# Two late stores of a batched matmul, each issued as three transfers over 112, 12 and 4 or 112, 8 and 8 partitions

## The chip, the core and the metric

The kernel runs on one core of a Trainium2 chip. The metric is the device time of one execution in microseconds, median of several executions. The core has a matrix engine (PE, whose weight loads are listed as PEld), three engines for elementwise work (DVE, ACT, POOL), a synchronising engine (SP), from whose queue all but one of this kernel's transfers are issued, and 16 DMA engines that carry out each transfer together. "DMA engine" below always means one of these 16.

## The reference

```python
def setup_inputs():
    batch, m, k, n = 16, 512, 1024, 768
    # x (16,512,1024), weight (1024,768), bias (768), residual (16,512,768), all float32, standard normal

def reference(x, weight, bias, residual):
    return (np.matmul(x, weight) + bias + residual).astype(np.float32)
```

So 8192 rows of x, each 1024 long, go through one 1024 x 768 weight; a bias row and a residual of the size of the output are added. In and out of the device memory go 33.6 MB of x, 3.1 MB of weight, 25.2 MB of residual and 25.2 MB of output.

## The kernel before

**Tiles.** The 8192 rows are cut into 64 tiles of 128 rows, eight tiles to a group, so there are eight groups g = 0 to 7. In a group each of the 128 partitions holds eight consecutive rows (`group`, "(p j) k -> p j k"): a partition of a group is one contiguous piece of 24,576 bytes in the output and the residual, and of 32,768 bytes in x. A group's store is therefore 128 pieces of 24,576 bytes, eight for each DMA engine.

**Work on one tile.** For tile t: ACT casts x to bf16 (`cast_x`, L121), PE transposes eight 128 x 128 blocks (L136), DVE copies them out of the accumulator memory (L143), PE makes 16 matmuls, eight blocks of the inner dimension times two column chunks of 512 and 256 (L150). DVE adds the residual to the result, in place in the residual's tile (`evacuate`, L167), and POOL adds the bias to it (`add_bias`, L174). The residual's tile then holds the output and is stored from there (`store`, L106). The first tiles are interleaved with the arrival of the weight, and group 0 has a tile of its own for the output; both lie at the other end of the kernel. The last tile is done in two column chunks, each with its own add (L296) and its own store.

**Order.** The order of each engine's instructions is written out by hand. The loop runs over t = 3 to 62; after tile t the dictionary `moves` says which loads and stores SP issues there. SP works its list strictly in order: an issue whose data is not ready holds all issues behind it. The list around the change is: load of residual 7 and store of group 4 (t = 45), store of group 5 (t = 47), store of group 6 (t = 55), and group 7 in five parts: tiles 0 to 3 (t = 59), 4 and 5 (t = 61), 6 (t = 62), then the last tile's 512 and 256 columns. Below they are called store 4, store 5, store 6, and 7a, 7b, 7c, 7d and 7e.

**Memory and waits.** Four places (`HOME`, "ring") hold the residuals in turn. Group 5 has place 2 and group 6 place 0, and no later load goes to either, so no load waits for stores 5 and 6. SP gives its transfers eight completion counters in turn; a transfer may be issued once the transfer eight places before it on SP's list has landed.

Of the kernel before, what the change touches and what calls it, by code (L numbers as in the profile page):

```python
# [10 lines left out]
P = 128  # L11
# [10 lines left out]
def kernel(  # L22
# [8 lines left out]
    nc = tc.nc  # L31
    x2d = x.flatten_outer_dims()
    res2d = residual.flatten_outer_dims()
    out2d = out.flatten_outer_dims()
# [7 lines left out]
    def group(ap, g):  # L42

        return ap[g * G * P:(g + 1) * G * P, :].rearrange("(p j) k -> p j k", p=P)
# [14 lines left out]
    def o(ins):  # L59
        return tc.keep_in_program_order(ins)  # L60
# [26 lines left out]
    x_tiles, r_tiles, o_tiles, w_stage = {}, {}, {}, {}  # L87
# [16 lines left out]
    def store(g, j0=0, j1=G, n0=0, n1=N):  # L104
        src = o_tiles[g] if g == 0 else r_tiles[g]
        o(nc.sync.dma_start(out=group(out2d, g)[:, j0:j1, n0:n1], in_=src[:, j0:j1, n0:n1]))  # L106


    xb_tiles, pt_tiles, xt_tiles, po_tiles = {}, {}, {}, {}
# [114 lines left out]
    for k in range(2, 6):  # L224
# [21 lines left out]
        5: [(load_r, 0), (load_r, 2)],  # L246
        12: [(load_x, 3)],
        15: [(store, 1)],
        17: [(load_r, 3)],
        20: [(load_x, 4)],  # L250
        21: [(load_r, 4), (store, 0)],
        28: [(load_x, 5)],
        29: [(load_r, 5), (store, 2)],
        36: [(load_x, 6)],
        37: [(load_r, 6), (store, 3)],
        44: [(load_x, 7)],
        45: [(load_r, 7), (store, 4)],
        47: [(store, 5)],
        55: [(store, 6)],
        59: [(store, 7, 0, 4)],  # L260
        61: [(store, 7, 4, 6)],
        62: [(store, 7, 6, 7)],
# [63 lines left out]
```

## Time and profile before

| | |
|---|---|
| time, median of 3 executions | 211.54 us (211.37 to 211.62) |
| the profiled execution: its time | 211.21 us |
| the profiled execution: span from the first to the last instruction | 209.4 us |
| granted clock of PE | 1.0 |
| bytes moved, mean rate over the span | 87.28 MB, 417 GB/s |
| store of a whole group: issue to landing, median of six | 23.8 us |
| 7a (1536 KB), 7b (768 KB), 7c (384 KB): issue to landing | 6.5, 5.7, 3.6 us |

A profile describes one execution. Its span is 1.8 us shorter than its time, which also holds what lies before the first and after the last instruction. "Busy" counts the time in which an engine works on an instruction; an engine can be busy all the time and still not be what the end waits for, and the reverse.

The DMA rows count what the 16 DMA engines do together. Behind them stand records of single packets (start, duration, bytes, queue) and, for every transfer, 16 times at which its completion counter rose, one for each DMA engine that has carried its share. Neither names the DMA engine. Since a DMA engine carries one packet after another, the end of one packet and the start of the next can be joined into 16 chains, and so a late DMA engine can be followed from transfer to transfer.

### The profile page before, as it was taken

Reading aid. Unit: us, or ns where it says so; the run is one execution under the profiler, and the core shown is the slowest. Engines: PE = TensorE matmul, PEld = TensorE weight load, DVE = VectorE, ACT = ScalarE, POOL = GpSimd, SP = SyncE. Lnnn points to the kernel's source line nnn. Section 1 sums busy time; section 2 is a strip of 40 time slices with the busy share of each in tenths; the row PEclk is TensorE's granted clock in tenths of the full one; section 3 lists DMA queues with packets and bytes.
Section 4 is the critical chain, followed back from the end, with each engine's and each line's share of the span. In section 5 each row is a group of like instructions: output and inputs, shape, how many; then the busy total and the mean of one; then the engine's idle time right before and its main releaser. Section 6 shows DMA issues by size and latency. Waiting matters only on the chain.

```text
span 209.4 us, 3673 instructions
## 1 busy us (share of the span) xinstructions
PE 199.8 (95%) x1560; PEld 134.1 (64%) x1590; DVE 113.9 (54%) x145; ACT 67.2 (32%) x69; POOL 109.1 (52%) x66
## 2 busy tenths in 40 slices
PE   7797999999999999999999999999999999999992
PEld 7554766666666666666666666666666666666661
DVE  0656555455477745464554454455445545579942
ACT  2633508606331073302632063310743008310000
POOL 2000000275579999966556655655665566554620
PEclk9999999999999999999999999999999999999999
DMA  6999999999999999999999999999999999999895
GB/s 232 402 424 440 448 404 444 419 451 413 418 468 430 410 418 430 443 432 419 427 437 432 426 421 440 444 426 427 413 441 448 426 421 407 437 443 432 355 403 222
DMA packets 5640, 87.28 MB, mean 417 GB/s; under 512 B 628, under 2 KB 756, under 8 KB 2296
## 3 DMA queue, kind: packets, MB, share of 16 engines
q1 hardware_dynamic: 5616, 87.03, 97.8%
q8 instruction: 12, 0.20, 0.4%
q14 instruction: 4, 0.03, 0.0%
q10 hardware_dynamic: 8, 0.01, 0.0%
HBM read 61.88 MB, written 25.17 MB: 416 GB/s over the span
## 4 chain that ended last, share of the span: by engine, by line
PE 88%; DMA 7%; issue 1%; DVE 1%; ACT 0%; SPq 0%; POOL 0%; POOLq 0%
PE po L150 74%; PE pt L136 13%; DMA x_tile<-in_x_dram 5%; DMA bias_rows<-in_bias_dram 3%; PE last_ps L293 1%; DVE xt L143 1%; ACT xb L118 0%; DVE r_tile L296 0%; SPq L97 0%; POOL ident masks.py:197 0%; POOL bias_rows L73 0%; POOLq L310 0%
## 5 line engine op out<-in xcount | busy, mean ns | idle before, releaser
L150 PE MATMUL po<-w_sb,xt 128*128 128x512 bf16 (+1 forms) x978 | 172.2, 324 | 3.2 <-DVE xt L143 1.5
L174 POOL TENSOR_TENSOR r_tile<-r_tile,bias_bc 128x768 f32<-128x768 f32 x53 | 95.7, 1813 | 90.4 <-DVE r_tile L167 90.4
L150 PEld LDWEIGHTS <-xt 128*128 128x128 bf16 x1008 | 95.8, 98 | 59.8 <-DVE xt L143 2.4
L121 ACT CAST xb<-x_tile 128x1024 bf16<-128x1024 f32 x62 | 62.1, 1044 | 109.2 <-DMA x_tile<-in_x_dram 58.2
L167 DVE TENSOR_TENSOR r_tile<-po,r_tile 128x768 f32<-128x768 f32 x55 | 52.6, 956 | 72.5 <-PE po L150 65.0
L143 DVE COPY xt<-pt 128x1024 bf16<-128x1024 bf16 x64 | 43.5, 680 | 3.9 <-PE pt L136 3.8
L136 PEld LDWEIGHTS <-xb 128*128 128x128 bf16 x512 | 35.3, 113 | 9.2 <-ACT xb L118 2.0
L136 PE MATMUL pt<-ident,xb 128*128 128x128 bf16 x512 | 39.0, 219 | 1.4 <-ACT xb L118 1.4
L178 POOL TENSOR_TENSOR o_tile<-o_tile,r_tile 128x768 f32<-128x768 f32 x6 | 12.1, 2056 | 0.0
L164 DVE TENSOR_TENSOR o_tile<-po,bias_bc 128x768 f32<-128x768 f32 x8 | 7.5, 953 | 4.8 <-PE po L150 4.8
L174 DVE TENSOR_TENSOR r_tile<-r_tile,bias_bc 128x768 f32<-128x768 f32 x3 | 6.6, 2189 | 0.0
L202 PE MATMUL warm_ps<-warm_in 128*128 128x128 bf16 x54 | 5.3, 281 | 1.1 <-DVE warm L76 1.1
L202 PEld LDWEIGHTS <-warm_in 128*128 128x128 bf16 x54 | 4.9, 133 | 1.1 <-DVE warm L76 1.1
L119 DVE CAST xb<-x_tile 128x512 bf16<-128x512 f32 x2 | 0.9, 427 | 6.5 <-DMA x_tile<-in_x_dram 6.5
L127 DVE CAST w_sb<-w_stage 128x768 bf16<-128x768 f32 x5 | 2.8, 558 | 2.6 <-DMA w_stage<-in_weight_dram 2.6
L178 DVE TENSOR_TENSOR o_tile<-o_tile,r_tile 128x768 f32<-128x768 f32 x2 | 3.9, 1944 | 0.0
L125 ACT CAST w_sb<-w_stage 128x768 bf16<-128x768 f32 x3 | 2.5, 832 | 4.1 <-DMA w_stage<-in_weight_dram 4.1
L293 PE MATMUL last_ps<-w_sb,xt 128*128 128x512 bf16 (+1 forms) x16 | 2.8, 326 | 0.0
L293 PEld LDWEIGHTS <-xt 128*128 128x128 bf16 x16 | 1.6, 98 | 1.1
L118 ACT CAST xb<-x_tile 128x512 bf16<-128x512 f32 x2 | 1.2, 618 | 3.1 <-DMA x_tile<-in_x_dram 3.1
L77 ACT ACT_TABLE_LOAD x1 | 1.3, 1283 | 2.6 <-POOL ident masks.py:199 2.6
L296 DVE TENSOR_TENSOR r_tile<-last_ps,r_tile 128x512 f32<-128x512 f32 (+1 forms) x2 | 1.1, 558 | 1.0 <-PE last_ps L293 1.0
(12 smaller groups left out, 3.1 us busy)
## 6 DMA issues: line engine op xcount, KB each, us to landing
x_tile<-in_x_dram SPq DMA_DIRECT2D x7, 4096.0 KB, 33.4
r_tile<-in_residual_dram SPq DMA_DIRECT2D x8, 3072.0 KB, 21.3
out_dram<-r_tile SPq DMA_DIRECT2D x6, 3072.0 KB, 23.8
x_tile<-in_x_dram SPq DMA_DIRECT2D x3, 1024.0 KB, 11.8
out_dram<-o_tile SPq DMA_DIRECT2D x1, 3072.0 KB, 31.2
w_stage<-in_weight_dram SPq DMA_DIRECT2D x6, 384.0 KB, 7.2
out_dram<-r_tile SPq DMA_DIRECT2D x1, 1536.0 KB, 6.5
x_tile<-in_x_dram SPq DMA_DIRECT2D x2, 512.0 KB, 8.2
```

The lines of the kernel that those rows point to most:

```text
L121: o(nc.scalar.copy(out=xb_tiles[t], in_=src))
L125: o(nc.scalar.copy(out=w_sb[:, k, :], in_=w_stage[0][:, k, :]))
L127: o(nc.vector.tensor_copy(out=w_sb[:, k, :], in_=w_stage[0][:, k, :]))
L136: o(nc.tensor.transpose(out=pt[:, k, :], in_=xb[:, h, j, :], identity=ident))
L143: o(nc.vector.tensor_copy(out=xt_tiles[t], in_=pt_tiles.pop(t)))
L150: o(nc.tensor.matmul(po_tiles[t][:, n0:n0 + nl], lhsT=xt_tiles[t][:, k, :], rhs=w_sb[:, k, n0:n0 + nl], start=(k == 0), stop=(k == n_k - 1),))
L164: o(nc.vector.tensor_add(out=o_tiles[0][:, j, :], in0=po, in1=bias_bc))
L167: o(nc.vector.tensor_add(out=rt, in0=po, in1=rt))
L174: o(engine.tensor_add(out=rt, in0=rt, in1=bias_bc))
L178: o(engine.tensor_add(out=ot, in0=ot, in1=r_tiles[0][:, t, :]))
L202: o(nc.tensor.matmul(warm_ps, lhsT=warm_in, rhs=warm_in, start=True, stop=True))
L293: o(nc.tensor.matmul(ps, lhsT=xt_tiles[t][:, k, :], rhs=w_sb[:, k, n0:n0 + nl], start=(k == 0), stop=(k == n_k - 1)))
```

## The change

Stores 5 and 6 are no longer one transfer over 128 partitions each, but three over neighbouring ranges of partitions: 0 to 111, 112 to 123 and 124 to 127 for group 5, and 0 to 111, 112 to 119 and 120 to 127 for group 6. Bytes, source, destination and place in SP's list stay; SP issues four more transfers. All else is as it was.

```diff
+    def store_by_partition(g, *bounds):
+
+        src, dst = r_tiles[g], group(out2d, g)
+        for (a, b) in zip(bounds, bounds[1:]):
+            o(nc.sync.dma_start(out=dst[a:b, :, :], in_=src[a:b, :, :]))
...
-        47: [(store, 5)],
-        55: [(store, 6)],
+        47: [(store_by_partition, 5, 0, 112, 124, P)],
+        55: [(store_by_partition, 6, 0, 112, 120, P)],
```

## The prediction

> **What bounds the kernel now.** I read the page first, then the chain of waits from its end, then a table of the last stretches, then SP's timeline, and last the completion records.
>
> ```profile
> PE 199.8 (95%) x1560; PEld 134.1 (64%) x1590; DVE 113.9 (54%) x145; ACT 67.2 (32%) x69; POOL 109.1 (52%) x66
> ...
> q1 hardware_dynamic: 5616, 87.03, 97.8%
> q8 instruction: 12, 0.20, 0.4%
> q14 instruction: 4, 0.03, 0.0%
> ...
> PE 88%; DMA 7%; issue 1%; DVE 1%; ACT 0%; SPq 0%; POOL 0%; POOLq 0%
> ...
> 202.94 2.61 PE last_ps L293 x16
> 205.56 0.02 issue
> 205.58 0.42 DVE r_tile L296
> ```
>
> PE sets the pace until 205.58 and waits for no transfer; the DMA engines are just as full (97.8%) without holding it. Stores 5 and 6 can reach the time only through what follows the last add at 206.00: 7e, and the packets still ahead of it.
>
> ```profile
> 190.00:195.00 5.00, 4.95 (x42) 3.35 (x42) 5.00 (x4) 0.00 (x0) 3.00 (x2) 1.00 1.00 426
> 195.00:200.00 5.00, 4.95 (x40) 3.33 (x40) 3.56 (x6) 0.00 (x0) 3.48 (x2) 1.00 0.83 351
> 200.00:205.00 5.00, 5.00 (x36) 2.98 (x34) 2.74 (x4) 0.00 (x0) 0.12 (x1) 1.00 0.97 404
> 205.00:210.00 5.00, 0.55 (x5) 0.24 (x3) 0.83 (x2) 0.00 (x0) 0.00 (x0) 0.96 0.44 169
> ```
>
> In 195 to 200 the DMA share (next to last column) falls to 0.83: some DMA engines have run dry while others still carry store 6. SP's timeline has the issues:
>
> ```profile
> 162.90 0.90 SPq L106 DMA_DIRECT2D out_dram<-r_tile  x2
> ...
> 184.53 0.33 SPq L106 DMA_DIRECT2D out_dram<-r_tile  x1
> ...
> 198.37 0.33 SPq L106 DMA_DIRECT2D out_dram<-r_tile  x1
> ```
>
> These are stores 4 and 5, store 6, and 7a. The completion records, 16 rises each, sorted (us):
>
> ```
> store 6  197.61 .63 .72 .86 198.26 .44 199.36 .37 .41 .60 .68 200.15 200.81 .83 201.19 201.22
> 7a       203.29 .30 .31 .32 .34 .35 .36 .40 .41 .44 .46 203.93 204.45 204.46 204.84 204.87
> 7e       207.62 .64 .66 .69 .69 .70 .75 .78 .80 .80 .82 .83 208.14 208.19 208.55 208.57
> ```
>
> Four DMA engines are late in all three rows and end the kernel; the span closes 0.84 us behind 208.57. From store 6 to 7e they take 7.35 us (208.57 − 201.22; 208.14 − 200.81 gives 7.33). The other twelve wait for issues and are through by 207.83. So an engine's last landing is its landing of store 6 plus 7.35, but not before 207.83: lateness counts from 200.48 on.
>
> Why they are late: joined into chains, the packets show the 12 instruction fetches (16 KB, 14.9 to 194.4, one each 16.3 us) going round eight DMA engines, so that four get two. A 24,576-byte packet takes 0.912 us and the next starts 4 ns earlier than its end, hence 0.908 a piece; a fetch takes 1.03 and stretches a neighbour to some 1.4, together 1.55 lost. Eight engines get none. One of those is late all the same: it takes 7.6 for a store's eight pieces where others take 7.27, and is the 200.15 above.
>
> **The change, part by part.**
>
> *Issues.* Four more on SP at 0.333 us (median on L106). After store 5's issue at 163.4 SP has nothing until 184.53, and after store 6's nothing until 198.37: two more issues in each gap cost 0; without the gaps, 1.33. Queued behind them is only 7a, which waits for POOL's adds. *New waits.* The counters come round sooner: 7c, 7d and 7e must find the three parts of store 5 landed, due by 194 against issues at 203.97, 205.43 and 206.04: 0, with over 9 us to spare. No load waits for these stores; PE, DVE and POOL keep their work.
>
> *Shares.* In before each engine has 16 pieces of stores 5 and 6. The 112 partitions go into 16 shares of seven. The small transfers have fewer partitions than there are engines. The trace has one such transfer, the bias row over four partitions: it left four packets of 3,072 bytes, and its counter rose for four landings after one jump, so it ran on four engines. I take the same for 4, 8 and 12: four engines carry 7+1+1+7+1+1 = 18 pieces, four 17, four 15, four 14.
>
> [...] The chains say this much: three of the bias's four engines are in the group that gets no fetch. So I let the 18 and 17 pieces fall on the eight without fetch.
>
> *Price of a small transfer's piece.* No row shows 24,576 bytes sent so. Low end: 0.908, side by side, as the first two bias packets (5.595 and 5.619, both 0.121, as long as weight packets of that size). High end: one after another within each four neighbours, 4 × 0.908 = 3.63; wholly one after another is excluded by these same two packets, which overlap by 0.097. What leaves it open is that every engine moves 27.1 GB/s, loads and stores alike (24,576 in 0.908; 32,768 in 1.210): the limit may be the engine, or the way into its eight partitions, and then small transfers crowd onto a few ways. The nearest row of two streams on one way is a packet beside a fetch: ten of 24,576 bytes, 1.30 to 1.46, mean 1.38. I take 1.38.
>
> [...]
>
> *Sum.* The four with 18 pieces: 14 × 0.908 + 4 × 1.38 = 18.23, against 16 × 0.908 = 14.53: +3.70. The quick ones of the eight without fetch land store 6 at up to 198.44 + 3.70 = 202.14 and 7e at 209.49: +0.92 against 208.57. If the slow one (200.15) is among the four, it lands at 203.85 and 211.20: +2.63. The trace doesn't say whether it is; I take the middle, +1.8. The profiled execution would come to 213.0; the median stands 0.33 above it, so **213.3 us**, own range 212.0 to 214.6.
>
> **Rivals.** *The shares even out.* Pieces cost 0.908 everywhere. The late four, with 14 pieces, land store 6 by 201.22 − 1.82 = 199.40, in time. The quick ones with 18 land by 200.26, also in time. The slow one with 17 lands at 201.06 and 7e at 208.41 (−0.16); had it no slowness in a split store, 207.83 would end it (−0.74). That gives 210.8 to 211.4. For it: slack and surplus fit piece by piece, and the bias's packets took their plain time. Against: the slow one eats most of it, and with 18 it lands at 201.97 and 209.32 (+0.75), which belongs to the forecast.
>
> *Neighbours queue for one way.* Mechanism: each four neighbouring partitions 112–115 to 124–127 pass one after another; it decides as soon as a piece costs more than about 1.5. Four engines take 14 × 0.908 + 4 × 3.63 = 27.23, +12.7. Store 6 then lands at 197.61 + 12.7 = 210.3 or a little later, 7e at 217.7 to 218.5: 220.6 to 221.5, say 221. For it: the constant 27.1 GB/s. Against: the bias row.
>
> *The surplus falls on the late four.* Then 201.22 + 1.82 + 7.35 = 210.39, +1.82: 213.4. For it: nothing in the records names an engine. Against: where three of the bias's packets went.
>
> **Chances.** About 0.2% (0.42 us) is what a measurement of this kernel can tell from no change. Forecast 0.37, all slower. Even shares 0.35: 0.30 faster (under 211.12), 0.05 same. Neighbours queue 0.19, slower. Surplus on the late four 0.09: 0.06 slower, and 0.03 same where the fetches of an execution begin elsewhere in their round. Faster 0.30, same 0.08, slower 0.62. The range 210.7 to 221.0 leaves out the best of the first rival and the worst of the second, under 0.2 together.
>
> **What would show it.** The first parts of stores 5 and 6 should end earlier by a piece and the pieces over 112 to 127 show 0.91, about 1.4, or about 3.6 us: that row alone separates forecast and rivals. The share in 195 to 200 would rise to about 1 if the shares even out. 7e's last landing sits at 207.8 to 208.4, near 210, or near 218. I am wrong if small transfers use all 16 engines, if SP's issues take more than their gaps, or if PE ends anywhere but at 205.6.

## The result and the profile after

The changed kernel takes 222.28 us (median of four executions, 221.77 to 222.57) against 211.45 us (also a median of four, one execution more than in the table of before): slower by a factor of 1.0505, 95% interval 1.0491 to 1.052. Ratios here and below leave out executions more than 1.5% slower than the fastest of the same kernel, which concerns two of the four of e3 and two of the four of e5. The profiled execution took 221.77 us with a span of 219.5 us; the span grew by 10.1 us.

The page of the changed kernel, its overview rows:

```profile
span 219.5 us, 3709 instructions
...
PE 201.7 (92%) x1590; PEld 134.3 (61%) x1590; DVE 114.3 (52%) x145; ACT 67.3 (31%) x69; POOL 109.1 (50%) x66
...
DMA  6999999999999999999999999999999999999961
GB/s 236 410 416 466 424 427 436 430 399 430 430 455 420 440 429 420 454 402 426 434 452 423 434 424 448 418 408 426 446 436 426 429 424 421 328 296 292 292 243 59
```

In the first 34 of the 40 slices the rate is about that of before. Then it falls from about 425 to about 290 GB/s and stays there until the last two slices, and all the while the DMA row shows 9: the DMA engines are busy, but each piece takes longer. The table of the last stretches says it more sharply (the last two columns are the DMA engines' mean busy share and the GB/s):

```profile
180.00:185.00 5.00, 5.00 (x43) 3.42 (x42) 1.96 (x4) 1.20 (x2) 3.27 (x2) 1.00 1.04 442
185.00:190.00 5.00, 5.00 (x39) 3.21 (x37) 5.00 (x6) 1.04 (x1) 2.43 (x2) 1.00 1.01 370
190.00:195.00 5.00, 5.00 (x43) 3.35 (x42) 5.00 (x4) 0.00 (x0) 3.00 (x2) 1.00 0.99 270
195.00:200.00 5.00, 5.00 (x41) 3.33 (x40) 3.57 (x6) 0.00 (x0) 3.48 (x2) 1.00 1.02 328
200.00:205.00 5.00, 5.00 (x36) 2.98 (x34) 2.74 (x4) 0.00 (x0) 0.12 (x1) 1.00 0.98 285
205.00:210.00 5.00, 0.55 (x5) 0.24 (x3) 0.83 (x2) 0.00 (x0) 0.00 (x0) 0.76 0.90 296
```

PE (third column) is as busy as before until 205 and then done: no compute moved. In 190 to 195 the engines moved 270 GB/s at a share of 0.99, where before they moved 426 at 1.00. The dry stretch of before (share 0.83 in 195 to 200) has gone, filled with slower pieces and not with more of them: of the 24,576-byte pieces that start after 185 us, the mean is 1.30 us against 0.918 before, the longest 4.68 us, and 93 of 235 take over 1.1 us (2 of 234 before). The small transfers of stores 5 and 6 have only 32 pieces, so at least 61 of these 93 belong to the transfers of 112 partitions or to the end of store 4: the large transfers are slowed too.

The lateness is handed to the last stores. The DMA issues, with median us from issue to landing:

```profile
out_dram<-r_tile SPq DMA_DIRECT2D x1, 1536.0 KB, 16.2
out_dram<-r_tile SPq DMA_DIRECT2D x1, 768.0 KB, 15.5
```

These are 7a and 7b, 6.5 and 5.7 us before. The completion records of the changed kernel:

```
store 5, 112   190.19 to 195.10, 16 landings
store 5, 12    one jump at 164.12, then 12 landings, 191.13 to 197.62
store 5, 4     one jump at 164.47, then 192.43 193.79 195.43 196.16
store 6, 112   199.26 to 207.74, 16 landings
store 6, 8     one jump, then 8 landings, 200.80 to 209.30
store 6, 8     one jump, then 201.77 203.45 205.03 207.67 .68 209.85 210.72 210.95
7e             211.25 ... 215.00 215.11 .12 217.29 218.15 218.39
```

Each small transfer ran on as many engines as it has partitions. The last part of store 5 lands at 197.62, where the whole of it had landed by 193.95 before. The engine that ends the kernel lands store 6 at 210.95 (201.22 before) and 7e at 218.39, 7.44 us later.

Joined into chains, the packets also show single pieces of the small transfers, as a piece with a completion packet directly before and behind it; 30 of the 32 can be told apart so. They took between 0.91 and 4.68 us, 2.1 in the mean. All 235 pieces together took 89 us longer than at 0.918 each; of that, 35 us lie in these 30, and so over half lies in the pieces of the large transfers.

### The profile page after: what moved, and what is told of

It is laid out like the page before. It is cut to its first block, busy times and chain, and to the rows that moved or that the text cites. A ratio compares the mean times of both kernels' runs of the same rounds, so it can differ in the third digit from the quotient of the medians.

```text
span 219.5 us, 3709 instructions
## 1 busy us (share of the span) xinstructions
PE 201.7 (92%) x1590; PEld 134.3 (61%) x1590; DVE 114.3 (52%) x145; ACT 67.3 (31%) x69; POOL 109.1 (50%) x66
## 4 chain that ended last, share of the span: by engine, by line
PE 85%; DMA 7%; DVE 1%; issue 0%; ACT 0%; SPq 0%; POOL 0%; POOLq 0%
PE po L156 71%; PE pt L142 12%; DMA x_tile<-in_x_dram 4%; DMA bias_rows<-in_bias_dram 3%; PE last_ps L299 1%; DVE xt L149 1%; ACT xb L124 0%; DVE r_tile L302 0%; SPq L97 0%; POOL ident masks.py:197 0%; POOL bias_rows L73 0%; POOLq L316 0%
## 5 line engine op out<-in xcount | busy, mean ns | idle before, releaser
L156 PE MATMUL po<-w_sb,xt 128*128 128x512 bf16 x1008 | 174.5, 326 | 1.5 <-DVE xt L149 1.1
```

The source lines that it names most:

```text
L156: o(nc.tensor.matmul(po_tiles[t][:, n0:n0 + nl], lhsT=xt_tiles[t][:, k, :], rhs=w_sb[:, k, n0:n0 + nl], start=(k == 0), stop=(k == n_k - 1),))
```

## The experiments

The diffs show each kernel against the changed one; e4 to e9 no longer hold its helper `store_by_partition`, and m1 and m2 are kernels of their own. WAYS stands for the second rival, that neighbouring partitions queue for one way; that partitions 32 away share it too is added in m1, as an assumption that nothing before that run had shown.

**Single stores (m1), a measurement of the disputed cost alone.**

```python
def store(a, n, step):                     # 17 sets, one after another
    between()                              # DVE writes one column, so the next store waits
    ...                                    # q goes on by n pieces of the output
    o(nc.sync.dma_start(out=pieces_out[q:q + n], in_=r_tile[a:a + (n - 1) * step + 1:step]))
```

> A kernel of its own: one residual group is loaded, then 17 stores of 24,576-byte pieces run one at a time (a small write by DVE between them), each from another set of partitions (first, number, step), all into neighbouring pieces of the output. It leaves out the matmul, the bias and most of the output. Theory WAYS (four neighbouring partitions, and those 32 away, share one way out of the on-chip memory that carries about 27 GB/s): a piece takes 0.91 us with 128 whole, 4 or 8 at step 4 (from 0 and from 64 alike); about 1.8 with 4 at step 32, 8 at step 16, 16 at step 8, 64 at step 1 or 2, 32 at step 1 or 4; the last of four neighbours ends after about 3.6 with 4, 8, 12 and 16 at step 1; 112 at step 1 between 0.91 and 1.8. Theory COUNT (a piece costs the same from anywhere, only the number of pieces of an engine matters): 0.91 in all sets. Theory SMALL (a transfer on fewer than 16 engines is slow in itself): 4, 8 and 12 slow at every step, 16, 32, 64 and 112 at 0.91. Theory MEMORY (the slowness is on the device-memory side): no difference between steps, since all write neighbouring pieces.

What the packet records gave (first partition, number, step; the whole transfer; the shortest, median and longest piece, us; the whole is from the first start to the last end):

```
0, 128, 1   7.50   0.91 0.92 0.95      112, 12, 1   3.90   3.42 3.60 3.77
124, 4, 1   3.84   3.42 3.55 3.60      0, 12, 4     1.94   0.91 1.65 1.70
0, 4, 4     0.98   0.91 0.91 0.91      112, 16, 1   3.92   3.42 3.57 3.78
0, 4, 32    1.93   1.78 1.83 1.88      0, 16, 8     1.99   1.59 1.76 1.92
120, 8, 1   3.85   3.42 3.68 3.77      0, 112, 1    9.04   0.91 0.92 2.12
0, 8, 4     0.98   0.91 0.91 0.91      0, 64, 1     7.78   1.77 1.91 1.92
64, 8, 4    0.97   0.92 0.92 0.92      0, 64, 2     3.84   0.91 0.92 0.96
0, 8, 16    1.91   1.69 1.82 1.89      0, 32, 1     3.95   1.77 1.90 1.93
                                       0, 32, 4     2.00   0.91 0.93 0.95
```

The table of stretches of the same kernel (DVE, POOL, PE clock, DMA share, GB/s) shows some of these sets: 128 whole; 4 neighbours; 4 at step 4; 4 at step 32; 8 at step 4; 64 neighbours; 64 at step 2.

```profile
12.00:19.70 7.70, 0.00 (x0) 0.00 (x0) 1.00 0.96 409
20.80:24.80 4.00, 0.00 (x0) 0.00 (x0) 1.00 0.22 25
26.60:27.70 1.10, 0.00 (x0) 0.00 (x0) 1.00 0.21 89
29.30:31.30 2.00, 0.00 (x0) 0.00 (x0) 1.00 0.23 49
38.30:39.40 1.10, 0.00 (x0) 0.00 (x0) 1.00 0.42 179
75.60:84.10 8.50, 0.00 (x0) 0.00 (x0) 1.00 0.89 185
85.60:89.60 4.00, 0.00 (x0) 0.00 (x0) 1.00 0.93 393
```

Rows two to four are the heart of the case. Four pieces, four engines, the same bytes, neighbouring targets, the same busy share of about 0.22 (four of sixteen engines, 0.25, less the edges of the stretch): 25, 89 and 49 GB/s. Only the set of partitions differs. Four neighbours hand out about one engine's rate between them (98,304 bytes in 3.84 us are 25.6 GB/s; a piece alone, 24,576 bytes in 0.91, 27.0); partitions 32 apart share as if two by two (1.83 us a piece in the median, twice 0.91). These three rows are as WAYS has them, the 32 away with it; COUNT, SMALL and MEMORY each fail on these three rows. The two sets where my expectation was off, 64 at step 2 and 32 at step 4, came out free of crowding at 0.92 and 0.93: I had worked out the shares as consecutive pieces, so they seem to be dealt out otherwise; how, no run here shows. Step 4 is not enough by itself: of 12 partitions at step 4, eight lie 32 apart in pairs, and the median is 1.65. The 112 alone took 9.04 us, longer than the whole 128, though seven pieces at 0.92 would be 6.4; 30 of its 112 pieces took over 1.1 us, the longest 2.12.

**One store at a time (e1, e2).**

```diff
-        55: [(store_by_partition, 6, 0, 112, 120, P)],
+        55: [(store, 6)],
```

> Store 5 split as in the change, store 6 whole. WAYS: four engines take 7 x 0.908 + 2 x 3.63 = 13.6 us for store 5 instead of 7.27, so they land store 6 at up to 204.8 and the end moves by about +3.5: 215. COUNT: +1.8 for these engines, inside their slack; if the slow engine is among them +0.8: 211.4 to 212.4. SMALL: as WAYS in time.

```diff
-        47: [(store_by_partition, 5, 0, 112, 124, P)],
+        47: [(store, 5)],
```

> Store 6 split as in the change, store 5 whole. WAYS: eight engines take 13.6 us instead of 7.27: about +3.5, 215. COUNT: +1.8 on eight engines, 211.4 to 212.4.

Measured: 218.16 us with store 5 split (216.63 to 219.53; ratio 1.0324, 1.0257 to 1.0391) and 217.82 with store 6 split (216.82 to 219.06; 1.030, 1.0259 to 1.0341), against 211.54. Each part alone costs +6.6 and +6.3 us, both together +10.8. COUNT is out; WAYS has the side right and the size too low by 3 us. In e1 the last part of store 5 lands at 199.82 (193.95 before), store 6 at 207.11 (201.22) and 7e at 214.54 (208.57): about 6 us late each time. What WAYS left out is the 112. The 24,576-byte pieces of e1 that start after 185 us took 51 us longer together than at 0.918 each, and 15 of the 16 small pieces, told apart by the chains (0.91 to 4.61 us, mean 2.6), hold 25 us of it; the rest lies in the pieces of the large transfers. A sum of the times measured alone does not give the size: 9.0 + 3.6 + 3.6 instead of 7.3 for the worst engine would make +7 at the end for one store, but about +16 for both, where the change took +10.8. By how much the pieces slow each other inside the kernel stays open.

**The same shares, still crowded (e3).**

```diff
-        47: [(store_by_partition, 5, 0, 112, 124, P)],
-        55: [(store_by_partition, 6, 0, 112, 120, P)],
+        47: [(store_by_partition, 5, 0, 112, P)],
+        55: [(store_by_partition, 6, 0, 112, P)],
```

> Stores 5 and 6 each split into 112 and 16 partitions: every engine keeps 7 + 1 = 8 pieces, so the shares are as even as before. COUNT: 211.5, no change. SMALL: 211.5, since both transfers run on 16 engines. WAYS: the 16 partitions hang on four ways, so a piece of theirs takes up to 3.63: +2.7 a store on every engine, +5.4 in all: about 217.

Measured: 218.41 to 224.97 us over four executions, median 221.58, ratio 1.038 (1.0314 to 1.0448). Every engine has eight pieces a store (7 + 1), as before, and the loss is +7 to +13 us, about that of the change and more than the +5.4 that WAYS gave. Unequal shares are not what costs.

**Even and odd, or lower and upper half (e4, e5).** In both, stores 5 and 6 are two transfers of 64 partitions; only the sets differ.

```diff
+    def store_sets(g, *sets, j0=0, j1=G):
+        src, dst = r_tiles[g], group(out2d, g)
+        for (a, n, step) in sets:
+            b = a + (n - 1) * step + 1
+            o(nc.sync.dma_start(out=dst[a:b:step, j0:j1, :], in_=src[a:b:step, j0:j1, :]))
...
-        47: [(store_by_partition, 5, 0, 112, 124, P)],
-        55: [(store_by_partition, 6, 0, 112, 120, P)],
+        47: [(store_sets, 5, (0, 64, 2), (1, 64, 2))],      # e5: (0, 64, 1), (64, 64, 1)
+        55: [(store_sets, 6, (0, 64, 2), (1, 64, 2))],      # e5: (0, 64, 1), (64, 64, 1)
```

> Stores 5 and 6 each as two transfers of 64 partitions, the even ones and the odd ones: every engine keeps 4 + 4 = 8 pieces, and by the single stores such a set moves at 0.92 us a piece. WAYS: no change, 211.2 to 211.9. Theory SPLIT (a store in several transfers over fewer than 128 partitions is slow beside other transfers, whatever the set): several us slower.

> The same with partitions 0 to 63 and 64 to 127: same number of transfers, pieces, bytes and shares as with the even and odd ones. WAYS: each transfer reaches half of the ways, a piece takes up to 1.9 where the 16 engines work on one half together and less where they are spread over both: between +1 and +14.6 for the two stores, I take 218. SPLIT and COUNT: as with the even and odd ones.

Even and odd: 211.48 us against 211.18 for the kernel before, run beside it, ratio 1.0011 (1.0000 to 1.0021). Lower and upper half: 225.65 us (222.63 to 228.21), ratio 1.0597 (1.0547 to 1.0648), 7.6 us above what I took and at the upper end of the bounds. The stretches of e4, and then of e5:

```profile
185.00:190.00 5.00, 5.00 (x40) 3.22 (x38) 5.00 (x6) 1.05 (x1) 2.37 (x2) 1.00 1.02 434
190.00:195.00 5.00, 5.00 (x43) 3.37 (x42) 5.00 (x4) 0.00 (x0) 3.07 (x2) 1.00 1.00 426
195.00:200.00 5.00, 5.00 (x40) 3.30 (x39) 3.58 (x5) 0.00 (x0) 3.40 (x2) 1.00 0.85 361
```

```profile
185.00:190.00 5.00, 5.00 (x39) 3.21 (x37) 5.00 (x6) 1.04 (x1) 2.45 (x2) 1.00 1.02 301
190.00:195.00 5.00, 5.00 (x43) 3.35 (x42) 5.00 (x4) 0.00 (x0) 3.00 (x2) 1.00 0.99 251
195.00:200.00 5.00, 5.00 (x41) 3.33 (x40) 3.58 (x6) 0.00 (x0) 3.47 (x2) 1.00 1.03 291
```

e4 is the picture of before; e5 has the full share at 251 to 301 GB/s, as the change has. Splitting a store is free, crowding is not: SPLIT is out, and this pair shows the cause inside the kernel itself.

**Unequal shares without crowding (e6, e7).**

```diff
-        47: [(store_by_partition, 5, 0, 112, 124, P)],
+        47: [(store, 5)],
-        55: [(store_by_partition, 6, 0, 112, 120, P)],
+        55: [(store_sets, 6, (0, 32, 4), (1, 32, 4), (2, 32, 4), (3, 8, 4), (35, 8, 4), (67, 8, 4), (99, 8, 4))],
```

> Store 5 whole; store 6 as three transfers of 32 partitions at step 4 and four of 8 partitions at step 4: eight engines carry 6 + 4 = 10 pieces of store 6, the other eight 6, so the shares are as uneven as in the change (18 against 14 over both stores), but in every transfer each engine has a way of its own. WAYS: pieces stay at 0.91 to 1.0 but for a few; the quick engines get +1.8 and stay in time, the slow one, if it has a surplus, lands at about 202 and ends the kernel at 209.3 of the span: 211.4 to 212.4. Theory SURPLUS (the loss is that four or eight engines have more pieces): about as slow as the change, 218 and more.

Measured: 212.77 us (212.62 to 212.91; ratio 1.0073, 1.0056 to 1.009), just above the bracket. The mean piece is 0.919 us, as before. With shares that were worked out to be as unequal as in the change the loss is 1.6 us (against 211.18) and not 10.8: SURPLUS is out.

In e7 store 6 is `store(6, 0, 4)` for tiles 0 to 3, and the seven sets of e6 with j0=4 for tiles 4 to 7.

> As the uneven store 6 before, but with half the surplus: tiles 0 to 3 of store 6 in one transfer of 128 partitions, tiles 4 to 7 in the three and four transfers of 32 and 8 partitions at step 4, pieces of 12,288 bytes. Eight engines get the bytes of one whole piece more, the eight that fetch get one less. WAYS: the late four come in at 200.3, in time; the slow one of the eight at 201.1, which ends the span at 208.4 + 0.84 instead of 208.57 + 0.84: 211.0 to 211.6, that is -0.3% to no change.

Measured: 211.63 us against 211.18 beside it, ratio 1.002 (1.0009 to 1.0032); no gain. The records show the intended evening-out, and what it is worth:

```
7e in e7  207.60 .61 .63 .65 .66 .66 .68 .68 .71 .71 .73 .75 .76 .77 .78   208.69
```

Fifteen engines are in time. One, the engine whose pieces are slow in stores (its landings of the parts of store 6 lie 0.96 to 1.00 us apart, those of the others about 0.91), has the surplus and now ends the kernel where the late four did.

**Four engines instead of eight (e8, e9).** In e8 the last two sets of e7 become four of 4 partitions, (67, 4, 4), (83, 4, 4), (99, 4, 4) and (115, 4, 4), and the first and third of its sets become one, (0, 64, 2).

> As the uneven half store 6, but the 16 half pieces that are moved off the fetching engines go to four engines (transfers of 4 partitions at step 4) instead of eight: these four get the bytes of two whole pieces more, the fetching eight of one less, the other four none. If the slow engine of the eight without fetch is not among the four: late four at 200.3, quick ones at 200.3, slow one at 200.15, all in time, the end at 207.8 + 0.84: 210.6 to 210.9. If it is: it lands at 202 and ends at 209.3: 212.0 to 212.4. SURPLUS would make it slower than the half surplus on eight by 1 us or more in either case.

Measured: 211.59 us, ratio 1.0009 (1.0001 to 1.0018), neither of the two cases. All 16 engines landed 7e between 209.12 and 209.31, as even as can be, but late: with this many transfers SP waited for completion counters, issued the last small one at 198.45 and 7a only at 200.30 instead of 198.37. e9 does the same in store 5 and leaves store 6 whole.

> The surplus for four engines, in the same sets and half pieces, moved from store 6 to store 5, store 6 whole, so that SP's waits for completion counters end long before 7a is due and 7a is issued at 198.4 again (in store 6 it came at 200.3, and the 16 engines then landed 7e within 0.2 us of each other, at 209.1 to 209.3). If the late four are all among the fetching engines relieved: the end at 207.8 + 0.84, 210.6 to 210.9. If the fetches of an execution begin elsewhere in their round, so that late engines get no relief or a surplus: 211.2 to 213. Mixed executions would spread over 210.6 to 213.

Measured: 212.01 us, ratio 1.0022 (1.0007 to 1.0038), spread over 211.31 to 212.71. 7a was issued on time, but the same waits put store 6's issue at 192.27 instead of 184.5, and engines ran dry before it. No version beat the kernel before.

**Loads (m2).** The same 17 sets with source and target exchanged.

> The 17 sets of the single stores as loads from the residual, one at a time, and one store; it leaves out the matmul, the bias and most of the output. WAYS on both directions: the same table as for the stores: 0.91 for 128, 4 and 8 at step 4, 64 at step 2, 32 at step 4; about 1.8 for 4 at step 32, 8 at step 16, 16 at step 8, 64 and 32 at step 1; 3.4 to 3.8 for 4, 8, 12, 16 at step 1. Only on the way out: 0.91 to 1.0 everywhere.

Pieces of 4 neighbours took 2.43 to 2.89 us, 4 at step 4 1.36 to 1.70; 64 neighbours 1.92 in the median and 64 at step 2 0.91. In these pairs the order is that of the stores. It is not so throughout: 4 at step 32 took 1.05 to 1.44, less than 4 at step 4. The factors are smaller, and the first pieces of every load are slow by themselves (up to 2.3 us in the whole 128), so that loads crowd by neighbours is likely from these rows, and the size and the pairs 32 apart stay open.

## Why the prediction was wrong, step by step

- **What bounds the kernel, and that the change can act only behind the last add:** right. PE ended at 205.6 again, and the whole loss lies behind it.
- **On how many engines a small transfer runs:** right; the counters rose 12, 4, 8 and 8 times.
- **An engine's last landing is its landing of store 6 plus 7.35:** right; 7.44, but from 210.95, where 202.14 to 203.85 had been worked out.
- **Price of a small transfer's piece:** this is the step that failed. "The nearest row of two streams on one way is a packet beside a fetch ... I take 1.38." Measured alone: 3.42 to 3.77 for 4, 8 and 12 neighbours, the high end that I had written down (3.63). Inside the changed kernel the small pieces took anything from 0.91 to 4.68, in the mean 2.1. A packet beside a fetch is two streams in one DMA engine, not four neighbours in four engines; as a row it was near in bytes and not in kind. The evidence I let speak for the low end, the bias's packets, was no test of it: a load of 3,072-byte pieces over partitions 32 apart, not a store from four neighbours.
- **The 112 at 0.908 a piece:** wrong too, and not thought of. I priced the small transfers and took the large one as plain. It alone takes 9.04 us, and in the changed kernel the pieces of the large transfers hold over half of the added 89 us. The first part of store 5 did not end earlier by a piece but at 195.10, after the 193.95 of the whole store before.
- **Surplus on the engines without fetch:** wrong in part. In the profile of e7 none of the late four is among the eight engines that the transfers of 8 partitions use; in that of e8 two of them are. So the late four do not stand to those eight alike in these two profiles, and a fixed surplus does not always meet them. The sum also let the small transfers fall on engines of the same set, so that four carry 18 pieces, four 17, four 15 and four 14; no run shows that term. The counters show 12, 4, 8 and 8 engines and not which, and what made the stores late was the time of the pieces (1.30 us in the mean after 185 us instead of 0.918), not their number (e6: 0.919 us a piece, +1.6 us).
- **Issues at 0 and new waits at 0:** right for the end, wrong in size. SP's two small issues of store 6 took 2.19 and 2.32 us instead of 0.333; the gap to 198.37 covered them. 7c, 7d and 7e took 1.78, 2.47 and 1.66 us to issue, and 7e went out at 208.40 instead of 206.04, but the last engine was still busy with the stores before it: from store 6 to 7e it took 7.44 us, as it had taken 7.35.
- **The rivals.** "Neighbours queue for one way", which had been given 0.19, is what the single stores show (four neighbours 3.55 us a piece in the median, four at step 4 0.91): 220.6 to 221.5 worked out, 222.28 measured. That the sum came so near is luck in good part: it priced every small piece at 3.63, above their mean in the kernel, and every piece of the 112 at 0.908, and for a single store (e1, e2) the same sum was 3 us too low. The DMA share of 1.02 in 195 to 200, named as the sign of even shares, came from slow pieces. Of the first rival e7 shows the mechanism (late four in time, slow engine last at 208.69 where 208.41 was worked out), with no time to gain.

## What to carry to other kernels

Before a transfer is cut by partitions, ask what each piece of its new set shares: in the stores of m1 four neighbours had about one DMA engine's rate between them (25.6 GB/s), and partitions 32 apart, as if two by two, as well (1.83 us a piece instead of 0.91). Sets of 4, 8 or 32 at step 4 and the even half kept the full rate (0.91 to 0.93 us a piece in the median), and the two halves cost nothing in e4 (ratio 1.0011); blocks of 4 to 64 neighbours (1.90 to 3.68) and the 112 (9.04 us whole instead of 6.4) did not, and the stores queued behind them paid (store 6 and 7e in e1, about 6 us each). The mark in the profile here was a full DMA share beside a fallen rate (0.99 at 270 GB/s in 190 to 195, before 1.00 at 426); the share alone would have looked like an improvement here.

## What was not expected of the hardware

- One engine's pieces take 0.94 to 0.98 us in stores 5 and 6 of before where the others take 0.91; its loads are not slower (1.21 us for 32,768 bytes, as the others). Why stays open.
- Issuing a transfer on SP took up to 2.47 us (7d) instead of 0.33 in the changed kernel, behind its split stores; in e6, 1.2 us for each of six. That was seen and not taken apart.
